# Recurrent mixer of a three-layer network: output products in runs, scores on 64 rows

## Chip, cores and metric

The kernel runs on one core of a Trainium2 chip. The metric is device time in microseconds: 3107.34 us, the median of 3 runs (3105.17 to 3111.62).

## What is computed

Input is a sequence of 512 tokens with 1024 features. A hybrid layer, an attention layer and a recurrent layer follow one another, each with an MLP. The change lies in the recurrent layer (RWKV-7), which runs over the tokens in both directions with 16 heads of 64 features each. Cut to its core:

```python
def rwkv7_scan(r, w, k, v, kk, a):
    def step(state, inp):
        r_t, w_t, k_t, v_t, kk_t, a_t = inp
        sa = jnp.einsum('bhvk,bhk->bhv', state, -kk_t)
        state = (state * w_t[:, :, None, :] + sa[..., None] * (kk_t * a_t)[:, :, None, :]
                 + v_t[..., None] * k_t[:, :, None, :])
        return state, jnp.einsum('bhvk,bhk->bhv', state, r_t)

for d in range(2):
    ...
    o = rwkv7_scan(*ins)
    ...
    dir_out.append((group_norm(o, gn_w, gn_b) + bonus.reshape(nB, S, D)) * g.astype(F32))
y = dir_out[0] + dir_out[1]
return y.astype(h.dtype) @ w_o
```

All of it is float32.

## The kernel before

The recurrent layer (`L3.rwkv`) takes the heads in pairs, so that one head lies on partitions 0 to 63 and the other on 64 to 127. A **unit** is one direction of one pair; there are 16, numbered 0 to 15 here. The 512 tokens of a unit are 8 chunks of 64. Three generators work on a unit:

- `prep` (L1265) makes the decays and the operands on DVE and ACT. Then come the **scores** (L1312): per head and chunk one product of `bk` (the chunk's b and k, 128 columns) with `ar`, masked by DVE (L1314) into `sc`. In `bk` the rows of the other head are zeros, so that each product has 128 rows. SP stores the diagonal blocks of the scores to DRAM (`lu`, L1321). PE also puts `bk` with tokens on the partitions (L1362, to `kb`).
- `invert` (L1367) reads `lu` back in another layout (`lt`, L1372, four DMAs) and inverts the triangular 32 x 32 blocks on POOL in 31 steps of two instructions (L1379, L1381). The result `x` goes out to DRAM (`xu`, L1388) and back into `X` (L1392), four DMAs each. `lt` and `x` have one buffer. PE finishes the 64 x 64 inverses (L1407, L1416).
- `scan` (L1423) builds the factors `m`, `n` (L1435 to L1457) and then runs the **chain** of states: per chunk one product a head (L1471) and one DVE instruction (L1472). Between the steps of the chain, `out` issues the **output** products of the chunk before into `po`: state products (L1465, 64 rows) and score-by-value products (L1467, 128 rows). The group norm (L1480 on), the gate and the sum follow. `lora2` (L1239) loads the gate's weight (128x128, one buffer) and splits it by ACT and DVE (L69, L70).

A loop over ticks advances every live generator by one step; a unit starts every 16 ticks, so that the scan of one unit, the inversion of the next and the preparation of the one after that run at the same time. Products of the values (L1207) and of the output weights (L1220) are mixed in. The emission order follows from the ticks, and a scheduling layer then places instructions on the queues; each engine and SP works through its own queue in order.

```python
for st, at in ((2, 36), (1, 9), (0, 0), (3, -4)):
    q, e = divmod(t - at, 16)
    if e == 0 and 0 <= q < NQ and not (st == 3 and q % 2):
        live.append((st, q, stages[st](q)))
```

Of the kernel before, what the change touches and what calls it, by code (L numbers as in the profile page):

```python
# [8 lines left out]
F32 = mybir.dt.float32  # L9
# [8 lines left out]
S = 512  # L18
# [6 lines left out]
class Core:  # L25
# [57 lines left out]
    def run(self, units, x, first=0, last=0, after=None, rate=1, segs=HALVES, before=None):  # L83
        """units: (weight AP [128, nk*128], consume(ps, s0, s1)); x[k] = (hi, lo) [128, S].
        The first and the last units run on half of the tokens at a time."""
# [22 lines left out]
    def final(self, units, x, put, g, then):  # L108
        """The last product of a block: put(m, a, ps) leaves tile m of its output in a; then
        h += norm(output) and the next norm start on one half of the tokens while the other half runs."""  # L110
# [26 lines left out]
    def ahead(self, gen, hp=HP):  # L137
        """The steps of gen, before what is already in the engines' queues."""
        if not hp:
            yield from gen  # L140
            return
        while True:
            with self.tc.high_priority(hp):
                try:
                    next(gen)
                except StopIteration:
                    return
            yield
# [15 lines left out]
    def prenorm(self, q, g, xn, s0, s1):  # L164
        """xn = h * rstd * g, split; q holds the squares of h."""
# [10 lines left out]
    def postnorm(self, y, q, g, s0, s1):  # L176
        """h += y * rstd * g; returns the squares of the new h."""
# [19 lines left out]
    def mlp(self, xn, g_post, w1, w2, ngrp, kind, then):  # L197
        """h += norm(act(xn @ w1) @ w2); w1(j) and w2(group, m) give packed weight APs."""
# [51 lines left out]
class SumSq:  # L250
    """Sum over the 1024 features (partitions of 8 tiles) of squares, spread over the partitions."""
# [59 lines left out]
class L1:  # L311
    """The hybrid mixer: sparse attention, spatial gating, RG-LRU, then the gated merge."""

    def l1_start(self, pool, xn, g):
        """Loads x and spawns the first norm; x is read again where it is added."""
# [65 lines left out]
    def branch(self, b, xn, x, merged, first=False):  # L381
        """merged += sigmoid(gate b) * (branch b @ its weights)."""
# [16 lines left out]
    # spatial gating  # L399

    def v_units(self, xn, v):
        """gelu(xn @ w_v) with the tokens on the partitions, 256 columns a step."""
# [61 lines left out]
    # RG-LRU  # L464
# [15 lines left out]
    def rglru(self, rg, xc):  # L480
        """Replaces each tile of xc by the recurrence's output."""
        nc, I = self.nc, self.I
        # rate = -8 softplus(-lam) = -8 (max(-lam, 0) + 2 atanh(e / (2 + e))), e = exp(-|lam|)
# [54 lines left out]
    # sparse attention: with 8 blocks and a window of the whole sequence, all three branches are causal  # L538

    def l1_attention(self, xn, g_pre, u, v):  # L540
        nc, tc, I = self.nc, self.tc, self.I
        yb = [self.accp.tile([128, S], F32, tag="acc", name="yb") for _ in range(NT)]
        with ExitStack() as cx:
# [27 lines left out]
            with tc.tile_pool(name="cm", bufs=1) as cm:  # L571
# [17 lines left out]
                def compress(which):  # L589
                    """The MLP over the blocks of 32 keys or values, 2 of a block's tokens at a time."""  # L590
# [89 lines left out]
            def compressed(hh, head, q, g, pct):  # L680
                """The branch over compressed blocks, for all of a head's queries."""
# [21 lines left out]
            def attend(pair, q, ks, vv, g):  # L703
                """A generator: the attention of a pair of heads of group g."""
# [104 lines left out]
class L2:  # L809
    """Dilated attention and windowed attention, then the output projection."""  # L810

    def bias_rows(self):
        """Bias of every distance and head, with the masks and the branches' multiplicities, in DRAM."""
# [16 lines left out]
    def q_split(self, ps, s0, s1, qst, scale, back=False):  # L830
        """Per head of a pair: its rows' high parts and, on the other 64 partitions, the low parts.
        With back the tokens run backwards."""
# [9 lines left out]
    def k_split(self, ps, s0, s1, krep):  # L842
        """Per head of a pair: high and low parts, each on both halves of the partitions."""
# [8 lines left out]
    def v_rows(self, vt, v):  # L852
        """v[:, b, :] = tokens of block b on the partitions."""
        nc = self.nc
        ps = self.pst.tile([128, 4, 128], F32, tag="tr", name="tr")
        for b in range(4):
            nc.tensor.transpose(ps[:, b, :], vt[:, b * 128:(b + 1) * 128], self.ident)
        nc.scalar.copy(v, ps)

    def l2_mixer(self, xn, g_post, then):  # L860
        nc, tc, I = self.nc, self.tc, self.I
        with ExitStack() as cx:
# [34 lines left out]
            def scores(pair, hh, qb, q, k, tb, win):  # L897
                """The weights of block qb of 128 queries of a head, which run backwards."""
# [29 lines left out]
            def attend(pair, q, ks, v, vc, win):  # L928
                """A generator: the attention of a pair of heads, in steps."""
# [80 lines left out]
class L3:  # L1010
    """The RWKV-7 mixer, in chunks of 64 tokens, both directions."""
# [19 lines left out]
    def l3_mixer(self, u, g_post, then):  # L1031
        nc, tc, I = self.nc, self.tc, self.I
        W = lambda n, i: I[n][i]
        with ExitStack() as lx:
# [3 lines left out]
            with tc.tile_pool(name="mx", bufs=8) as mx:  # L1038
# [5 lines left out]
                def blend(c, i, t, s0, s1):  # L1044
                    """A mix of the tokens before, at and after."""
# [82 lines left out]
    def rwkv(self, lp, rkd, vm, tw, ta, sg):  # L1128
        nc, tc, I = self.nc, self.tc, self.I
        with ExitStack() as cx:  # L1130
            pool = lambda n, b, **kw: cx.enter_context(tc.tile_pool(name=n, bufs=b, **kw))
            arp, vsp, bkp, unp, sp, wk = (pool(n, b) for n, b in (
                ("ar", 4), ("vs", 3), ("bk", 1), ("un", 1), ("s3", 2), ("wk", 2)))
# [24 lines left out]
            def head_scale(sq, fn):  # L1158
                """PSUM [128, S]: fn(sum over each head's 64 rows of sq), on all rows of the head."""
# [24 lines left out]
            def w4(i):  # L1184
                """A 4 KB tile out of the weights' slots."""
# [7 lines left out]
            # b and k, scaled by the inverse decays: (b, k) of the first head above zeros, (k, b) of the second below zeros  # L1193
            bk = bkp.tile([128, 2, 8, 2, 64], F32, tag="bk", name="bk")
            nc.gpsimd.memset(bk, 0.0)
# [3 lines left out]
            def values(p):  # L1199
                """The values of a pair of heads."""  # L1200
# [10 lines left out]
            def output(p):  # L1211
                """Adds a pair of heads' part of the output product."""
# [37 lines left out]
            def pair(p):  # L1250
                """What the two directions of a pair of heads share."""
# [16 lines left out]
            def prep(q, C):  # L1268
                """Decays, scores and the other operands of one direction of a pair of heads."""
# [24 lines left out]
                ar0, ar1 = ar[:, 0], ar[:, 1]  # L1294
                nc.vector.tensor_tensor(c8(ar0), c8(flip(kk, d)), dp[:, :, 0:64], op=ALU.mult)
                for h, rw, ow in H:
                    nc.vector.tensor_tensor(bk[rw, h, :, h, :], c8(al)[rw], c8(s)[rw], op=ALU.mult)
                yield
                nc.vector.tensor_tensor(kd, flip(k[p], d), kd, op=ALU.mult)
                for h, rw, ow in H:  # L1300
                    nc.vector.tensor_tensor(bk[rw, h, :, 1 - h, :], c8(kd)[rw], c8(s)[rw], op=ALU.mult)  # L1301
# [3 lines left out]
                sc = C["sc"] = []  # L1305
                for h, rw, ow in H:
                    sc.append(w4(h).rearrange("p (c t) -> p c t", c=8))
                    for g in range(2):
                        ps = self.psm.tile([128, 4, 2, 64], F32, tag="mm", name="mm")
                        for c in range(4):  # L1310
                            cc = 4 * g + c
                            nc.tensor.matmul(ps[:, c], bk[:, h, cc].rearrange("p a t -> p (a t)"),  # L1312
                                             ar[:, :, cc * 64:(cc + 1) * 64], start=True, stop=True)
                        nc.vector.tensor_tensor(sc[h][:, 4 * g:4 * g + 4, :], ps.rearrange("p c a t -> p c (a t)"),  # L1314
# [8 lines left out]
                # bonus, and the values centred over the head with the tokens on the partitions  # L1323
# [33 lines left out]
                # tokens on the partitions  # L1357
                kb = C["kb"] = w4(q % 2).rearrange("p (h c t) -> p h c t", h=2, c=8)
                for h, rw, ow in H:
                    ps = mm()  # L1360
                    for c in range(8):
                        nc.tensor.transpose(ps[:, c, :], bk[rw, h, c].rearrange("p a t -> p (a t)"),  # L1362
# [4 lines left out]
            def invert(q, C):  # L1367
                """Inverses of the 32 x 32 diagonal blocks: (quarter of the rows, unit) on the partitions;
                then the 64 x 64 ones."""
# [27 lines left out]
                # off-diagonal blocks: -X1 U12 X2  # L1397
# [25 lines left out]
            def scan(q, C):  # L1423
                """The recurrence of the states as S' = d (M S + n), one product a chunk, and the outputs
                S^T Q + [u0; v]^T scores; then the group norm and the gate."""
# [35 lines left out]
                def out(c):  # L1461
# [233 lines left out]
```

## Time and profile before

| | |
|---|---|
| median of 3 runs | 3107.34 us |
| profiled execution: span of its instructions | 3102.4 us |
| its own launch time | not listed by itself; the median is 4.9 us above the span |
| busy, share of the span | PE 95%, DVE 54%, ACT 43%, POOL 13% |
| recurrent stage | about 2031 to 2684 us |
| sum over 2028 to 2712 us | PE 611.3, DVE 369.8, ACT 273.1, POOL 360.8 us busy of 684 |

Busy shares are means over stages with different limits, so the stage is read by its own stretches, waits and timelines. In the rows below, x counts executed records; a float32 product of PE is two records. PEclk is the mean granted clock of TensorE as a share of 2.4 GHz. A row marked SPq is an issue of a DMA on SP's queue, PE a matmul. Times are from the span's start.

### The profile page before, as it was taken

What the parts mean: (1) busy time and instruction counts of PE and PEld (TensorE: products, weight loads), DVE (VectorE), ACT (ScalarE), POOL (GpSimd) and SP (SyncE); (2) the same over time, 40 slices, a digit from 0 to 9 for tenths busy, and PEclk for the clock granted to TensorE, in tenths of its full rate; (3) what the DMA queues carried; (4) which work ended last, traced back from release to release, by engine and by line L of the source; (5) the groups of instructions that cost most, each with busy time, mean ns of one, the idle gap of its engine ahead of it and who ended that gap; (6) DMA issues with size and microseconds to landing.
All of it is one profiled execution on the core that took longest, in us unless ns stands there. A gap on an engine that the chain in (4) does not pass through costs nothing.

```text
span 3102.4 us, 49534 instructions
## 1 busy us (share of the span) xinstructions
PE 2957.2 (95%) x19720; PEld 2382.2 (77%) x19720; DVE 1675.8 (54%) x3427; ACT 1344.1 (43%) x2450; POOL 397.6 (13%) x1117
## 2 busy tenths in 40 slices
PE   7999999999999999999999999979999999699998
PEld 7877778778888889777988897757666666488887
DVE  5566684553553335757733357855545555553345
ACT  5566652663443223555532235644444443243232
POOL 0000000000000000000000000045555555100000
PEclk9999999999999999999999999987889998899999
DMA  4301122223223223222222232311111111212231
GB/s 142 99 29 48 42 96 89 95 95 119 90 77 106 94 94 99 75 75 64 76 94 93 93 127 88 109 45 35 42 48 49 49 47 36 85 61 95 95 108 42
DMA packets 139415, 243.99 MB, mean 79 GB/s; under 512 B 62064, under 2 KB 82288, under 8 KB 139056
## 3 DMA queue, kind: packets, MB, share of 16 engines
q1 hardware_dynamic: 136864, 238.90, 24.5%
q8 instruction: 155, 2.54, 0.3%
q10 hardware_dynamic: 2320, 1.93, 0.2%
q14 instruction: 76, 0.62, 0.1%
HBM read 228.13 MB, written 12.65 MB: 78 GB/s over the span
## 4 chain that ended last, share of the span: by engine, by line
PE 80%; DVE 7%; POOL 4%; issue 3%; ACT 3%; DMA 2%; SPq 1%; POOLq 0%; ACTq 0%; DVEq 0%
PE mm L80 56%; PE fil L1207 2%; POOL x L1381 2%; POOL tmp L1379 2%; PE mm L1312 2%; PE fil L1220 2%; PE o L1467 2%; PE o L732 1%; PE mm L416 1%; PE o L1465 1%; PE mm L1090 1%; PE tr L722 1%; PE o L950 1%; PE mm L1248 1%; PE mm L761 1%
## 5 line engine op out<-in xcount | busy, mean ns | idle before, releaser
L80 PE MATMUL mm<-xh,wh 128*128 128x512 f32 (+1 forms) x2072 | 739.7, 358 | 10.7 <-ACT xh L69 6.6
L80 PE MATMUL mm<-xl,wh 128*128 128x512 f32 (+1 forms) x2072 | 736.5, 357 | 0.3 <-DVE xl L70 0.3
L80 PE MATMUL mm<-xh,wl 128*128 128x512 f32 (+1 forms) x2072 | 733.0, 355 | 2.1 <-DVE wl L65 2.1
L63 ACT CAST wh<-wr 128x1024 fp32r<-128x1024 f32 (+1 forms) x343 | 357.0, 1044 | 755.8 <-PE mm L80 612.1
L65 DVE TENSOR_TENSOR wl<-wr,wh 128x1024 fp32r<-128x1024 f32 (+1 forms) x343 | 416.6, 1216 | 458.8 <-ACT wh L63 448.9
L80 PEld LDWEIGHTS mm<-xh,wh 128*128 128x128 f32 x2072 | 392.7, 190 | 73.8 <-ACT xh L69 7.9
L80 PEld LDWEIGHTS mm<-xh,wl 128*128 128x128 f32 x2072 | 392.4, 190 | 60.8 <-issue 3.5
L80 PEld LDWEIGHTS mm<-xl,wh 128*128 128x128 f32 x2072 | 392.5, 190 | 56.6 <-issue 3.3
L80 PE MATMUL mm<-hl,wh 128*128 128x512 f32 (+1 forms) x880 | 304.9, 347 | 0.0
L80 PE MATMUL mm<-hh,wh 128*128 128x512 f32 (+1 forms) x880 | 303.6, 346 | 0.0
L80 PE MATMUL mm<-hh,wl 128*128 128x512 f32 (+1 forms) x880 | 303.5, 345 | 0.0
L1379 POOL TENSOR_TENSOR tmp<-x,lt 128x60 f32<-128x60 f32 (+24 forms) x496 | 170.6, 344 | 172.9 <-DMA lt<-lu 135.4
L275 POOL TENSOR_TENSOR r<-r,mhalf 128x2 f32<-128x2 f32 x24 | 24.1, 1003 | 1291.0 <-DVE r L274 1291.0
L80 PEld LDWEIGHTS mm<-hl,wh 128*128 128x128 f32 x880 | 166.4, 189 | 22.4 <-DVE hl L70 0.5
L80 PEld LDWEIGHTS mm<-hh,wl 128*128 128x128 f32 x880 | 166.2, 189 | 21.8
L80 PEld LDWEIGHTS mm<-hh,wh 128*128 128x128 f32 x880 | 166.1, 189 | 21.9
L1381 POOL TENSOR_TENSOR x<-x,tmp 128x60 f32<-128x60 f32 (+24 forms) x496 | 173.8, 350 | 38.9
L241 DVE TENSOR_TENSOR acc<-acc,mm 128x256 f32<-128x256 f32 (+1 forms) x88 | 47.4, 541 | 178.7 <-PE mm L80 178.7
L265 DVE TENSOR_TENSOR sqa<-sqa,sq 128x256 f32<-128x256 f32 x182 | 75.2, 421 | 56.1 <-ACT sq L264 52.2
L69 ACT CAST hh<-t 128x512 fp32r<-128x512 f32 (+1 forms) x106 | 57.0, 539 | 77.5 <-DVE t L212 68.4
L674 DVE CUSTOM_DVE_ANT_0 s<-mm,cmask 128x128 f32<-128x128 f32 (+3 forms) x128 | 59.9, 487 | 47.0 <-PE mm L756 23.1
L1312 PE MATMUL mm<-ar,bk 128*128 128x128 f32 x512 | 68.6, 291 | 15.1 <-DVE bk L1301 7.9
(399 smaller groups left out, 5010.1 us busy)
## 6 DMA issues: line engine op xcount, KB each, us to landing
wr<-in_mlp_w_dram SPq DMA_DIRECT2D x128, 512.0 KB, 3.5
wr<-in_w_ffn_in_dram SPq DMA_DIRECT2D x44, 512.0 KB, 3.5
wr<-in_w_mg_dram SPq DMA_DIRECT2D x24, 512.0 KB, 3.6
wr<-in_w_br_dram SPq DMA_DIRECT2D x24, 512.0 KB, 3.5
wr<-in_attn_w_in_dram SPq DMA_DIRECT2D x18, 512.0 KB, 3.6
wr<-in_w_ffn_out_dram SPq DMA_DIRECT2D x16, 512.0 KB, 3.5
lt<-lu SPq DMA_DIRECT2D x64, 128.0 KB, 2.6
wr<-in_w_kv_dram SPq DMA_DIRECT2D x12, 512.0 KB, 4.0
```

Of the source, the lines that this page charges most:

```text
L63: nc.scalar.copy(hi, raw)
L65: nc.vector.tensor_tensor(lo, raw, hi.bitcast(F32), op=ALU.subtract)
L69: self.nc.scalar.copy(hi, src)
L80: nc.tensor.matmul(ps, l, r[:, s0:s1], start=(n == 0), stop=(n == 3 * nk - 1))
L265: nc.vector.tensor_tensor(self.acc, self.acc, t, op=ALU.add)
L674: nc.vector.tensor_tensor_reduce(s, ps, mask, -1.0, 3e38, ADD, ALU.min, m)
L1207: nc.tensor.matmul(ps, w[:, i * 128:(i + 1) * 128], vm[i], start=(i == 0), stop=(i == NT - 1))
L1220: nc.tensor.matmul(ps, w[:, m], ys[p], start=True, stop=True)
L1312: nc.tensor.matmul(ps[:, c], bk[:, h, cc].rearrange("p a t -> p (a t)"), ar[:, :, cc * 64:(cc + 1) * 64], start=True, stop=True)
L1379: nc.gpsimd.tensor_tensor(t, x[:, :m, i:i + 1].to_broadcast([128, m, n]), lt[:, i:i + 1, i + 1:].to_broadcast([128, m, n]), op=ALU.mult)
L1381: nc.gpsimd.tensor_tensor(x[:, :m, i + 1:], x[:, :m, i + 1:], t, op=ALU.subtract)
L1467: nc.tensor.matmul(po[rw, c], sc[h][:, c, 64:128], vs[:, c, h, :], start=(c == 0), stop=True, skip_group_check=True)
```

## The change

Three edits. (1) `bk` holds both heads on their own 64 rows, (b, k) for the first and (k, b) for the second, without zeros; it is made anew per unit with two buffers, and the memset goes. A score product now reads 64 rows, and the products of the two heads follow each other chunk by chunk into two PSUM tiles. (2) All score-by-value products of a unit stand in one run ahead of the chain, with one more tick. (3) The state products follow the chain in the text. Elsewhere the diff takes out comments and docstrings only.

```diff
-                ("ar", 4), ("vs", 3), ("bk", 1), ("un", 1), ("s3", 2), ("wk", 2)))
+                ("ar", 4), ("vs", 3), ("bk", 2), ("un", 1), ("s3", 2), ("wk", 2)))
...
-            bk = bkp.tile([128, 2, 8, 2, 64], F32, tag="bk", name="bk")
-            nc.gpsimd.memset(bk, 0.0)
...
+                bk = bkp.tile([128, 8, 2, 64], F32, tag="bk", name="bk")
                 for h, rw, ow in H:
-                    nc.vector.tensor_tensor(bk[rw, h, :, h, :], c8(al)[rw], c8(s)[rw], op=ALU.mult)
+                    nc.vector.tensor_tensor(bk[rw, :, h, :], c8(al)[rw], c8(s)[rw], op=ALU.mult)
...
-                sc = C["sc"] = []
-                for h, rw, ow in H:
-                    sc.append(w4(h).rearrange("p (c t) -> p c t", c=8))
-                    for g in range(2):
-                        ps = self.psm.tile([128, 4, 2, 64], F32, tag="mm", name="mm")
-                        for c in range(4):
-                            cc = 4 * g + c
-                            nc.tensor.matmul(ps[:, c], bk[:, h, cc].rearrange("p a t -> p (a t)"),
-                                             ar[:, :, cc * 64:(cc + 1) * 64], start=True, stop=True)
-                        nc.vector.tensor_tensor(sc[h][:, 4 * g:4 * g + 4, :], ps.rearrange("p c a t -> p c (a t)"),
+                sc = C["sc"] = [w4(h).rearrange("p (c t) -> p c t", c=8) for h in range(2)]
+                for g in range(2):
+                    ps = [self.psm.tile([128, 4, 2, 64], F32, tag="mm", name="mm") for _ in range(2)]
+                    for c in range(4):
+                        cc = 4 * g + c
+                        for h, rw, ow in H:
+                            nc.tensor.matmul(ps[h][:, c], bk[rw, cc].rearrange("p a t -> p (a t)"),
+                                             ar[rw, :, cc * 64:(cc + 1) * 64], start=True, stop=True)
+                    for h in range(2):
+                        nc.vector.tensor_tensor(sc[h][:, 4 * g:4 * g + 4, :], ps[h].rearrange("p c a t -> p c (a t)"),
                                                 mask.unsqueeze(1).to_broadcast([128, 4, 128]), op=ALU.mult)
...
-                def out(c):
-                    cs = slice(c * 64, (c + 1) * 64)
+                for c in range(8):
                     for h, rw, ow in H:
-                        if c:
-                            nc.tensor.matmul(po[rw, c], ar1[rw, cs], n[rw, c - 1, :], start=True, stop=False,
-                                             skip_group_check=True)
-                        nc.tensor.matmul(po[rw, c], sc[h][:, c, 64:128], vs[:, c, h, :], start=(c == 0), stop=True,
+                        nc.tensor.matmul(po[rw, c], sc[h][:, c, 64:128], vs[:, c, h, :], start=(c == 0), stop=False,
                                          skip_group_check=True)
+                yield
                 for c in range(1, 7):
...
-                    out(c - 1)
                     yield
-                out(6)
-                out(7)
+                for c in range(1, 8):
+                    for h, rw, ow in H:
+                        nc.tensor.matmul(po[rw, c], ar1[rw, c * 64:(c + 1) * 64], n[rw, c - 1, :], start=False, stop=True,
+                                         skip_group_check=True)
```

The queues move at two places that the prediction speaks of. The first is SP's queue around the gap after unit 8 (lines in the changed program stand 1 to 3 lower; `lora_dram 128x128` is the gate's weight). Before:

```order
L1214 DMA wr<-in_rk_w_o_dram 128x8x128
L1254 DMA k<-rkd 128x512
L1255 DMA r<-rkd 128x512
L1388 DMA xu<-x 256x1x32 x2
L1321 DMA lu<-wh 32x8x32 x2
L1388 DMA xu<-x 256x1x32 x2
L1241 DMA w_22618<-in_rk_lora_dram 128x128
L1321 DMA lu<-wl 32x8x32 x2
L1241 DMA w_23078<-in_rk_lora_dram 128x256
L1392 DMA X<-xu 32x8x32 x4
L1372 DMA lt<-lu 32x1024 x4
```

And in the changed program:

```order
L1238 DMA w_23079<-in_rk_lora_dram 128x256
L1251 DMA k<-rkd 128x512
L1252 DMA r<-rkd 128x512
L1238 DMA w_22633<-in_rk_lora_dram 128x128
L1387 DMA xu<-x 256x1x32 x4
L1320 DMA lu<-wh 32x8x32 x2
L1320 DMA lu<-wl 32x8x32 x2
L1391 DMA X<-xu 32x8x32 x4
L1371 DMA lt<-lu 32x1024 x4
```

The four xu now stand together, the lu behind them, and both weights have moved ahead of xu.

The second is PE's queue at the start of the last unit's chain (sc is the chain's PSUM tile, o the outputs'). Before:

```order
L1471 MATMUL sc_25482<-n,m 64x64 x2
L1467 MATMUL o_25481<-vs,wh 64x64
L1467 MATMUL o_25481<-vs,wl 64x64
L1465 MATMUL o_25481<-n,ar 64x64
L1467 MATMUL o_25481<-vs,wh 64x64
L1465 MATMUL o_25481<-n,ar 64x64
L1471 MATMUL sc_25482<-n,m 64x64 x2
L1467 MATMUL o_25481<-vs,wl 64x64
L1465 MATMUL o_25481<-n,ar 64x64
L1467 MATMUL o_25481<-vs,wh 64x64
L1465 MATMUL o_25481<-n,ar 64x64
L1467 MATMUL o_25481<-vs,wl 64x64
```

And in the changed program, from the end of the run of 16 score-by-value products:

```order
L1463 MATMUL o_25495<-vs,wh 64x64
L1463 MATMUL o_25495<-vs,wl 64x64
L1468 MATMUL sc_25496<-n,m 64x64 x2
L1473 MATMUL o_25495<-n,ar 64x64 x2
L1468 MATMUL sc_25496<-n,m 64x64 x2
L1473 MATMUL o_25495<-n,ar 64x64 x2
L1468 MATMUL sc_25496<-n,m 64x64 x2
L1473 MATMUL o_25495<-n,ar 64x64 x2
```

The score-by-value products (L1463) have left the chain; the state products (L1473) stand between its steps in pairs, and four come behind the last step.

## Rows read from the trace of the kernel before

**Rows 1.** Busy time by stretch: engine busy us (x instructions), PEclk, DMA share, GB/s.

```profile
2180.00:2218.00 38.00, 31.81 (x415) 24.68 (x414) 19.35 (x37) 20.48 (x35) 21.87 (x64) 0.77 0.16 40
2370.00:2408.00 38.00, 37.98 (x485) 27.36 (x485) 23.99 (x49) 14.35 (x27) 21.43 (x59) 1.00 0.19 46
```

**Rows 2.** Waits from 2020 to 2720 us: engine, line, releaser; us, times, longest.

```profile
POOL tmp L1379 <- DMA lt<-lu: 135.4, 16, 36.5
POOL x L1374 <- DMA xu<-x: 70.9, 15, 5.4
```

**Rows 3.** Waits of SP's own queue from 2100 to 2600 us, same columns.

```profile
SPq L1388 <- POOL x L1381: 186.9, 12, 27.3
SPq L1321 <- DVE n L1472: 2.0, 4, 1.3
```

**Rows 4.** Timeline of POOL, units 8, 9, 15: start us, us, engine, line, op, tiles.

```profile
2345.55 0.24 POOL L1379 TENSOR_TENSOR tmp<-x,lt 128x31 f32<-128x31 f32 x1 [6.90 <-DMA lt<-lu]
...
2377.74 0.40 POOL L1374 COPY x<-xeye 128x256 f32<-128x256 f32 x1 [5.36 <-DMA xu<-x]
...
2385.50 0.24 POOL L1379 TENSOR_TENSOR tmp<-x,lt 128x31 f32<-128x31 f32 x1 [6.90 <-DMA lt<-lu]
...
2393.28 0.29 POOL L1379 TENSOR_TENSOR tmp<-x,lt 128x60 f32<-128x60 f32 x1
...
2401.64 0.62 POOL L1379 TENSOR_TENSOR tmp<-x,lt 128x60 f32<-128x60 f32 x1
...
2622.27 0.24 POOL L1379 TENSOR_TENSOR tmp<-x,lt 128x31 f32<-128x31 f32 x1 [7.94 <-DMA lt<-lu]
...
2645.97 0.21 POOL L1381 TENSOR_TENSOR x<-x,tmp 128x8 f32<-128x8 f32 x1
```

**Rows 5.** Timeline of SP's issues in the gaps after units 5 and 8.

```profile
2255.39 2.90 SPq L1388 DMA_DIRECT2D xu<-x  x4
...
2262.64 1.73 SPq L1372 DMA_DIRECT2D lt<-lu  x4
...
2372.40 1.22 SPq L1388 DMA_DIRECT2D xu<-x  x2
...
2376.36 0.53 SPq L1241 DMA_DIRECT2D w<-in_rk_lora_dram  x1
...
2381.34 1.78 SPq L1372 DMA_DIRECT2D lt<-lu  x4
```

**Rows 6.** Timeline of PE in the stage: scores, a run of products, alternating products.

```profile
2327.98 1.95 PE L1312 MATMUL mm<-ar,bk 128*128 128x128 f32 x16
2329.86 1.03 PE L1445 MATMUL mm<-vs,wh 128*64 128x64 f32 x28
...
2336.18 0.33 PE L1467 MATMUL o<-vs,wh 128*64 128x64 f32 x2
2336.44 0.32 PE L1465 MATMUL o<-n,ar 64*64 64x64 f32 x2
```

**Rows 7.** Timeline of DVE near the end of unit 8's inversion.

```profile
2370.09 0.68 DVE L1314 TENSOR_TENSOR wh<-mm,const 128x512 f32<-128x512 f32 x1
2370.69 0.34 DVE L70 TENSOR_TENSOR w<-w,w 128x128 fp32r<-128x128 f32 x1
```

**Rows 8.** Timeline of the last unit's chain of states, PE, DVE and ACT.

```profile
2665.93 0.33 PE L1471 MATMUL sc<-n,m 64*64 64x64 f32 x4
...
2668.97 0.33 PE L1471 MATMUL sc<-n,m 64*64 64x64 f32 x4
...
2669.36 0.28 DVE L1472 SCALAR_TENSOR_TENSOR n<-sc,dl,n 128x64 f32<-128x64 f32 x1 [1.27 <-PE sc L1471]
...
2671.93 0.48 PE L1471 MATMUL sc<-n,m 64*64 64x64 f32 x4
...
2672.46 0.28 DVE L1472 SCALAR_TENSOR_TENSOR n<-sc,dl,n 128x64 f32<-128x64 f32 x1 [1.54 <-PE sc L1471]
...
2677.30 0.60 ACT L1480 ACTIVATE t<-o 128x512 f32<-128x512 f32 x1 [13.67 <-PE o L1467]
```

More of the change, by code (lines that the diff above doesn't have):

```diff
@@ L1300, in prep @@
                 for h, rw, ow in H:
-                    nc.vector.tensor_tensor(bk[rw, h, :, 1 - h, :], c8(kd)[rw], c8(s)[rw], op=ALU.mult)
+                    nc.vector.tensor_tensor(bk[rw, :, 1 - h, :], c8(kd)[rw], c8(s)[rw], op=ALU.mult)
                 nc.vector.tensor_tensor(c8(ar1), c8(flip(r[p], d)), dp[:, :, 1:65], op=ALU.mult)
@@ L1361, in prep @@
                     for c in range(8):
-                        nc.tensor.transpose(ps[:, c, :], bk[rw, h, c].rearrange("p a t -> p (a t)"),
+                        nc.tensor.transpose(ps[:, c, :], bk[rw, c].rearrange("p a t -> p (a t)"),
                                             self.ident[rw, rw])
```

## Prediction

> **What bounds the kernel now.** I read three views in this order: the busy time by stretch, who waits for whom, and the timelines of POOL and SP. All of the change lies in the recurrent mixer, where PE seems to be the limit: from 2370 to 2408 us it is busy 37.98 of 38 us [rows 1]. The waits say otherwise. There are 16 units (a direction of a pair of heads, 0 to 15). Per unit POOL inverts triangular blocks in 62 instructions, and between two inversions it waits first for the store of its result (xu), then for the next unit's input (lt) [rows 2]. SP, which issues both, waited in its queue almost only for POOL's result; for scores (lu) it waited 2.0 us behind the costliest entry [rows 3]. So a ring closes without PE: POOL inverts, SP issues xu, X and lt in turn, POOL starts again. For unit 8 the inversion runs from 2345.55 until xu is issued at 2372.40 (26.8 us), and the next starts at 2385.50: a gap of 13.1 us, 12.3 of them waits and the rest POOL's own work [rows 4, 5]. Over the 15 gaps: (135.4 - 36.5 for the first unit + 70.9) / 15 + 0.9 = 12.2 us [rows 2]. A period is thus about 39 us, with no instruction of PE in it.
>
> The test is a stretch in which PE has less to do. From 2180 to 2218 it is busy only 31.8 of 38 us, at a mean granted clock of 0.77 [rows 1], and POOL is as busy (21.9 against 21.4 us). PE idling or not, the ring turns alike. What PE saves inside the ring is therefore covered by the inversion. Three places remain: the start, SP's part of the ring, and the tail after the last inversion.
>
> **PE's saving, and what it is worth inside.** *Scores.* 32 records of 128 columns (two records per product) take 2 x 1.95 us a unit [rows 6]. On 64 rows, with the heads taken alternately, I expect two products side by side: 1.95 us saved, or 0 if they run one after another. *Scan.* 30 output products a unit change the array's shape from one to the next, one every 0.26 us (2336.18 to 2336.44): 30 x 0.26 = 7.8 us. In one run the same kind costs 1.03 / 28 = 0.037 us a record, so 60 records are 2.2 us; with about eight changes of shape left at 0.26 - 0.07 = 0.19 it is 3.7 us. Saved: 4.1 us. Together 6 us a unit, 97 us over 16 units. All of it is hidden in the ring; if that cover were gone it would show in full (first rival).
>
> **The start.** Unit 0's scores stand ahead of the ring. PE finishes up to 1.95 us sooner, but DVE must still mask four tiles, now two at a time. Bounds 0 and 1.95 us. A mask takes 0.68 us [rows 7]: two finished tiles after 0.97 us and four masks give 3.7 us, where four tiles at 0.97 us and the last mask give 4.6. I take 0.9.
>
> **SP's part of the ring.** The change moves more than it says. In the gap after unit 8, SP issues two xu, two lu, two xu, a small weight, two lu, another weight, then X and lt. In the changed order four xu stand first, and both weights have moved ahead of them, under the inversion. What this is worth is read from unit 5, which has the good order already: from xu to lt 2262.64 - 2255.39 = 7.25 us, against 2381.34 - 2372.40 = 8.94 [rows 5]. A clean gap is then 13.1 - 1.7 = 11.4 us, 0.8 under the mean. In the changed program ten of the 15 gaps have xu first (after units 4 to 9 and 11 to 14), though three of these keep a weight inside (0.53 us of issue); after units 2, 3 and 10 the xu are still split, and after unit 1 the lu move ahead of the ring. I take ten times 0.7, 7 us. Bounds: 0, if the stretching of single issues takes it back, and 13, if every one of the ten has been at 12.7.
>
> Moved past on SP are also the loads of k, r and the output weights, now ahead of xu in several units. They wait for slots that PE, ACT or DVE free, and behind them waits the ring; see the third rival.
>
> **The tail.** Behind the last inversion nothing hides PE. The last unit's chain takes from 2665.93 to 2677.30, 11.4 us [rows 8], with outputs between its six steps. After: a run of 32 score records, 32 x 0.037 = 1.2 us. Then six steps, each from PE's start to DVE's start 0.39, DVE 0.28, and back to PE at least 0 and at most the same 0.39, of which I take 0.1: 0.77, so 4.6 us, with the state products inside them; the last four products 0.3. That is 6.1 us, 5.3 less. At the lower clock a step is 0.53 + 0.28 + 0.1 = 0.9 us, and with the products doubled I get 8.4 us, 3.0 less. The same four records grow from 0.33 to 0.48 us between 2669 and 2672, and with less work before them they may stand at the lower clock from the first step. I take 4.3 between. The Trainium skill ("TensorE: Matmul & The Clock Gate", section "HAM oscillation — how this bites in real kernels") warns of just this: pauses of TensorE bring its clock down, so saved work can be paid back in rate. By it the sum would take the 3.0; [rows 1] agree with it: 0.77 where PE idles, 1.00 where it does not.
>
> **Sum.** 0.9 + 7 + 4.3 = 12.2 us. The profiled span is 3102.4 us, 4.9 under the median of 3107.3; so 3090.2 in the profile and **3095.1 us** as median. From the bounds: 0 + 0 + 3 = 3 us to 2 + 13 + 5.3 = 20 us saved, 3087 to 3104. A measurement of this kernel tells 0.2% (6.2 us) from no change.
>
> **Rivals.** *First, PE is the bound after all.* For: the full stretch of [rows 1]. Against: the ring of [rows 2, 3], in which PE has no part. Time: 97 + 4 us less, 3006. Chance 0.05.
>
> *Second, POOL gives it back.* The inversion is not of one length: 26.8 us for unit 8, 23.9 for unit 15, behind which no preparation runs [rows 4]. One form of POOL's takes 0.29 us at 2393 and 0.62 at 2401, while DVE prepares a unit. If PE is ready sooner, DVE's work gathers right behind X, inside the inversion, and its own waiting moves into the gap. The dearest case is that all of DVE's work falls inside: 2.9 us go with what now overlaps, some 27/39 of it, so at most 2.9 x 12/27 = 1.3 us a unit, 19 us. A typical half, 10 us, leaves 12.2 - 10 = 2 us: 3105, no change. The Trainium skill ("SBUF — State Buffer", section "Who interferes with whom") gives the rule: a VectorE instruction with two SBUF inputs holds up a GpSimd instruction that reads SBUF. [...] Chance 0.18.
>
> *Third, slower: a load holds up SP.* In the gaps after units 4, 6, 8, 12 and 14 a small weight (128x128) now stands directly ahead of xu, and it waits until DVE has split the weight before it. In unit 8 that split ends at 2371.03 [rows 7], 1.4 us before xu at 2372.40. The point that decides is the inversion's end: each us by which the split comes later lengthens the ring by one. If in these five units it came 6 us behind the inversion, 30 us are added, and 3107.3 + 30 - 12 = 3125. Against it: what leads to the split is PE work of the unit before, which gets shorter by up to 6 us. Chance 0.05.
>
> *That the change doesn't do what it says*, the 64-row products not running side by side, alters only the start and stays inside the forecast.
>
> **Numbers.** The forecast has 0.72, the rivals 0.05, 0.18 and 0.05. The range 3085 to 3106 holds the forecast with both its bounds and most of the second rival; outside lie the first, the third and the worst of the second. Faster by over 0.2% (below 3101.1): nine tenths of the forecast, the first rival, and a sixth of the second: 0.65 + 0.05 + 0.03 = 0.73. Slower: the third, and a little of the second: 0.06. Between: 0.21.
>
> **What would show it.** Right: PE's busy time in the stage falls by 60 us or more while POOL's inversions keep their 26 to 27 us and 62 instructions; xu to lt takes 7.3 to 8 us; the last chain ends within 9 us; the output products lie in runs at under 0.05 us a record. Score records start at half the spacing where heads alternate; equal spacing would show that step wrong. Wrong altogether would be a period far below 36 us (PE or DVE had set it), or SP waiting at the small weight with xu's data ready.

## Result and the profile after

| | before | after |
|---|---|---|
| median, runs taken side by side | 3106.26 us (4 runs, 3104.9 to 3111.62) | 3078.55 us (4 runs, 3076.38 to 3079.8) |
| span of the profiled execution | 3102.4 us | 3074.6 us |

The ratio is 0.991, interval 0.989 to 0.993: 27.7 us less, where the prediction had 12.2. The direction was right; the time lies 6 us below the low end of the range.

The busy time by stretch, in the changed kernel (columns as in [rows 1]); the last row is the stretch of the table of before, 611.3 us of PE there:

```profile
2180.00:2218.00 38.00, 25.60 (x431) 20.05 (x431) 17.50 (x36) 18.27 (x33) 20.58 (x64) 0.81 0.20 49
2360.00:2398.00 38.00, 27.76 (x293) 17.16 (x293) 18.05 (x35) 13.97 (x23) 22.91 (x66) 0.78 0.16 39
2028.00:2712.00 684.00, 538.83 (x7260) 390.04 (x7259) 386.91 (x774) 296.38 (x538) 352.31 (x1026) 0.84 0.20 51
```

PE lost 72.5 us of busy time in the stage, and in 17 stretches of 38 us from 2040 us on it is busy for 36.1 us at most (37.98 before); POOL is about as busy as before (352.3 us, before 360.8). The waits of POOL from 2020 to 2720 us and of SP from 2100 to 2600 us, against [rows 2, 3]:

```profile
POOL tmp L1378 <- DMA lt<-lu: 120.1, 14, 39.0
POOL x L1373 <- DMA xu<-x: 67.9, 15, 6.0
...
SPq L1387 <- POOL x L1380: 169.1, 10, 23.6
SPq L1387 <- POOL X L1384: 88.3, 4, 29.4
SPq L1320 <- DVE n L1469: 0.7, 2, 0.4
```

They read as before: POOL waits for xu, then lt, SP for POOL. One inversion and the gap behind it (POOL, then SP, then the masks of the next unit on DVE), unit 8 as in [rows 4, 5]:

```profile
2339.82 1.35 POOL L1378 TENSOR_TENSOR tmp<-x,lt 128x31 f32<-128x31 f32 x1 [7.14 <-DMA lt<-lu]
...
2364.75 0.21 POOL L1380 TENSOR_TENSOR x<-x,tmp 128x8 f32<-128x8 f32 x1
2369.01 0.40 POOL L1373 COPY x<-xeye 128x256 f32<-128x256 f32 x1 [4.05 <-DMA xu<-x]
...
2376.05 0.24 POOL L1378 TENSOR_TENSOR tmp<-x,lt 128x31 f32<-128x31 f32 x1 [6.18 <-DMA lt<-lu]
```
```profile
2364.99 2.52 SPq L1387 DMA_DIRECT2D xu<-x  x4
2367.62 1.03 SPq L1320 DMA_DIRECT2D lu<-wh  x2
2368.74 0.89 SPq L1320 DMA_DIRECT2D lu<-wl  x2
2369.90 1.78 SPq L1391 DMA_DIRECT2D X<-xu  x4
2371.84 1.72 SPq L1371 DMA_DIRECT2D lt<-lu  x4
```
```profile
2352.24 0.69 DVE L1313 TENSOR_TENSOR wh<-mm,const 128x512 f32<-128x512 f32 x1 [0.52 <-PE mm L1310]
2352.85 0.68 DVE L1313 TENSOR_TENSOR wl<-mm,const 128x512 f32<-128x512 f32 x1
```

The inversion takes 25.1 us, the gap 11.1 (26.8 and 13.1 before); xu to lt is 6.9 us. The last mask is done at 2353.5, 11.4 us ahead of the inversion's end. Now the same masks in the kernel before, where this inversion ended at 2372.4 [rows 5]:

```profile
2372.92 0.69 DVE L1314 TENSOR_TENSOR wl<-mm,const 128x512 f32<-128x512 f32 x1
2373.81 0.69 DVE L1314 TENSOR_TENSOR wl<-mm,const 128x512 f32<-128x512 f32 x1 [0.20 <-PE mm L1312]
```

They came 2.1 us **after** the end, and waited for PE's scores. The prediction never compared these two times.

Worked out from the timelines of POOL, DVE and ACT, over the whole stage:

| us | before | after | change |
|---|---|---|---|
| stage's first norm (kk) to the first inversion | 21.5 | 22.2 | +0.6 |
| 16 inversions | 421.2 | 410.7 | -10.5 |
| 15 gaps | 182.6 | 171.2 | -11.5 |
| last inversion's end to the square of the outputs (ACT) | 31.1 | 25.7 | -5.4 |
| median end of the last mask against the inversion's end, units 7 to 14 | 0.0 | -9.9 | |

These parts are 26.8 of the spans' 27.8 us. The rest lies ahead of kk (+1.0) and behind the tail (-2.0), in code that is the same; over all profiles of this study kk begins between 2019.4 and 2024.7 us, and what follows the tail takes 422.7 to 425.1, so nothing is read into it.

The tail, PE, DVE and ACT in the last unit's chain ([rows 8] before):

```profile
2645.55 0.27 PE L1463 MATMUL o<-vs,wh 128*64 128x64 f32 x1
...
2646.64 0.33 PE L1468 MATMUL sc<-n,m 64*64 64x64 f32 x4
2647.02 0.28 DVE L1469 SCALAR_TENSOR_TENSOR n<-sc,dl,n 128x64 f32<-128x64 f32 x1 [0.73 <-PE sc L1468]
2647.36 0.33 PE L1468 MATMUL sc<-n,m 64*64 64x64 f32 x4 [0.27 <-DVE n L1469]
...
2650.95 0.48 PE L1473 MATMUL o<-n,ar 64*64 64x64 f32 x4 [0.27 <-DVE n L1469]
2651.48 0.60 ACT L1478 ACTIVATE t<-o 128x512 f32<-128x512 f32 x1 [8.32 <-PE o L1473]
```

From the run of outputs to ACT 5.9 us, a step 0.72 us.

### The profile page after: what moved, and what is told of

The parts are those of the page before. It is cut to its first block, busy times and chain, and to the rows that moved or that the text cites. A ratio compares the mean times of both kernels' runs of the same rounds, so it can differ in the third digit from the quotient of the medians.

```text
span 3074.6 us, 49553 instructions
## 1 busy us (share of the span) xinstructions
PE 2859.1 (93%) x19720; PEld 2302.1 (75%) x19720; DVE 1671.7 (54%) x3427; ACT 1356.4 (44%) x2460; POOL 386.7 (13%) x1116
## 4 chain that ended last, share of the span: by engine, by line
PE 74%; POOL 9%; DVE 6%; issue 4%; DMA 3%; ACT 2%; SPq 2%; POOLq 0%; ACTq 0%; DVEq 0%
PE mm L80 57%; POOL x L1380 4%; POOL tmp L1378 4%; PE o L732 1%; PE mm L416 1%; PE mm L1090 1%; PE tr L722 1%; PE o L950 1%; PE fil L1204 1%; DMA lt<-lu 1%; PE mm L761 1%; PE tr L924 1%; DVE sqa L265 1%; PE mm L903 1%; SPq L1391 1%
## 5 line engine op out<-in xcount | busy, mean ns | idle before, releaser
L80 PEld LDWEIGHTS mm<-hh,wh 128*128 128x128 f32 x880 | 166.2, 189 | 21.8
L241 DVE TENSOR_TENSOR acc<-acc,mm 128x256 f32<-128x256 f32 (+1 forms) x88 | 47.4, 541 | 178.3 <-PE mm L80 178.3
L70 DVE TENSOR_TENSOR hl<-t,hh 128x512 fp32r<-128x512 f32 (+1 forms) x106 | 62.2, 589 | 35.3 <-ACT hh L69 34.6
```

Source lines behind the costliest of these rows:

```text
L70: self.nc.vector.tensor_tensor(lo, src, hi.bitcast(F32), op=ALU.subtract)
L80: nc.tensor.matmul(ps, l, r[:, s0:s1], start=(n == 0), stop=(n == 3 * nk - 1))
L241: nc.vector.tensor_tensor(a, a, ps, op=ALU.add)
```

## Experiments

Eleven kernels ran, each beside the kernel before on one chip. In e1 to e4 the prediction's **ring** stood against **PE** (the gain is a share of what PE saved). Their results led to a third theory, **two limits**: before the change PE's work and the ring of POOL and SP were of equal length from unit 7 on, so each took back what the other was given; the change freed PE, and the ring alone remained.

| run | median us | ratio to before, interval | inversions / gaps, us | last mask, units 7 to 14 |
|---|---|---|---|---|
| e1 scores edit alone | 3109.87 | 0.9998, 0.9986 to 1.001 | 412.0 / 200.6 | +4.0 |
| e2 scan edit alone | 3083.74 | 0.9909, 0.9895 to 0.9923 | 415.6 / 173.9 | -8.2 |
| e3 before, half of POOL's steps | 3079.06 | 0.9899, 0.988 to 0.9918 | | |
| e4 after, half of POOL's steps | 2971.60 | 0.9549, 0.9536 to 0.9562 | | |
| e5 before, lu on ACT's queue | 3110.80 | 1.0013, 0.9999 to 1.0026 | 420.7 / 183.6 | +3.1 |
| e6 after, lu on ACT's queue | 3092.81 | 0.9958, 0.9945 to 0.997 | 418.5 / 178.3 | -4.7 |
| e7 after, two buffers, lu and lt on ACT | 3125.03 | 1.0065, 1.0051 to 1.0078 | 422.3 / 208.0 | -0.6 |
| e8 after, one-input products | 3043.33 | 0.9797, 0.9782 to 0.9812 | 383.4 / 170.5 | -8.9 |
| e9 after, lu first | 3033.68 | 0.9754, 0.9733 to 0.9776 | 412.5 / 125.0 | -2.5 |
| e10 after, ring open | 3078.41 | 0.9894, 0.9874 to 0.9914 | 421.4 / 162.2 | +3.1 |
| e11 before, lu first | 3124.40 | 1.0047, 1.003 to 1.0065 | 415.7 / 204.9 | +5.8 |

(Last column: median end of a unit's last mask against the end of the running inversion; plus is late.)

### Which edit: e1 and e2

e1 is the changed kernel with the scan's old text, e2 the kernel before with the new scan and the old scores.

> The scores edit alone: the scan keeps its old text, outputs between the steps of the chain. SP's queue has the four xu together in 13 of 15 gaps, as in the full change. Theory 'ring' (POOL's inversion and SP's issues set the period, the tail is separate): the gaps shrink by 7 to 12 us, the inversions by some us, the last chain stays at 11.4 us; 10 to 17 us less than before, 3089 to 3096. Rival 'PE' (PE's readiness sets the period, and the gain is a share of PE's saved time): the scores give about a quarter of the 72 us that PE saved, so a quarter of the 28 us: 7 us less, 3099, whatever SP's order is.

> The scan edit alone: outputs in one run and behind the chain, scores as before on 128 rows with zeros. xu stays split by lu in 8 of the gaps. Theory 'ring': the tail gives 5.4 us, the gaps 0 to 4 us and the inversions 0 to 5 us: 6 to 12 us less, 3094 to 3100. Rival 'PE': three quarters of the saved PE time lie here, so three quarters of the 28 us, about 21 us less, 3085.

The scan edit alone gives the whole gain, some 28 us, where PE's share had three quarters of it; the scores edit gives none, which neither theory had. In e1 the scores took PE 45.0 us in the stage (2028 to 2712 us) instead of 68.6, but PE's busy time there stayed the same, 610.9 us (611.3 before), at a lower granted clock, 0.82 instead of 0.85. From 2300 to 2500 us PE was full at 0.81 (0.91 before, first of the four rows of the next section):

```profile
2300.00:2500.00 200.00, 196.45 (x2107) 132.91 (x2106) 106.75 (x210) 77.23 (x140) 107.34 (x318) 0.81 0.17 44
```

So PE gained nothing from the smaller scores there; why the clock was lower is not shown. e1 has the four xu together, and its inversions are as short as in the changed kernel, but its gaps add up to 200.6 us. From unit 7 on the masks are late. The worst gap, behind unit 7's inversion, on POOL, SP and DVE:

```profile
2326.52 0.21 POOL L1380 TENSOR_TENSOR x<-x,tmp 128x8 f32<-128x8 f32 x1
2338.32 0.40 POOL L1373 COPY x<-xeye 128x256 f32<-128x256 f32 x1 [11.59 <-DMA xu<-x]
2348.88 0.24 POOL L1378 TENSOR_TENSOR tmp<-x,lt 128x31 f32<-128x31 f32 x1 [9.69 <-DMA lt<-lu]
```
```profile
2333.80 0.33 SPq L1238 DMA_DIRECT2D w<-in_rk_lora_dram  x1
2334.22 2.52 SPq L1387 DMA_DIRECT2D xu<-x  x4
2339.07 1.63 SPq L1320 DMA_DIRECT2D lu<-wh  x2
```
```profile
2338.95 0.68 DVE L1313 TENSOR_TENSOR wl<-mm,const 128x512 f32<-128x512 f32 x1
```

SP stands at the gate's weight until 2333.8, and xu comes 7.5 us late: the third rival, here and, by 2.1 us, behind unit 9. Then lu waits for a mask that ends at 2339.6, 12.9 us behind the inversion. This gap is 22.2 us. With the masks late, the better order on SP bought nothing.

### Which limit: e3 and e4

```diff
                 for i in range(31):
+                    if i % 2 == 0:
+                        continue
                     m, n = i // 4 + 1, 31 - i
```

> The kernel before with every second step of POOL's inversion left out (15 of 31 steps remain, so the states are computed from a wrong inverse). Each inversion becomes some 13 us shorter. Theory 'ring': the period falls from 39.2 us until PE is full; PE's busy time is 554 of the ring's 604 us, at a mean clock of 0.85, so 45 to 90 us less, 3015 to 3060. Rival 'PE' (PE paced the stage before): under 15 us less, above 3090.

> The changed kernel with the same steps left out. Theory 'ring': the period falls until PE is full, and PE's busy time is 470 of 582 us: 100 to 150 us less than the changed kernel, 2930 to 2980, so the change is worth 70 to 95 us once POOL is out of the way. Rival 'PE': the change already got what PE had to give; the two kernels with half of the steps stand 28 us apart as the full ones do.

Half of the steps are some 16 x 13 = 208 us of POOL. Before the change this brought 32 us, between the two expectations; after it 107 us, as the ring had it, and the two stand 107.5 us apart instead of 28. PE from 2300 to 2500 us says why. In the fence: before, changed kernel, e3, e4.

```profile
2300.00:2500.00 200.00, 193.62 (x2246) 137.28 (x2246) 113.84 (x220) 82.44 (x151) 114.40 (x320) 0.91 0.19 49
```
```profile
2300.00:2500.00 200.00, 174.46 (x2382) 117.82 (x2381) 122.82 (x238) 93.72 (x167) 119.39 (x341) 0.90 0.20 51
```
```profile
2300.00:2500.00 200.00, 196.10 (x2298) 137.53 (x2298) 113.10 (x222) 82.18 (x149) 48.74 (x160) 0.91 0.19 48
```
```profile
2300.00:2500.00 200.00, 194.49 (x2915) 136.74 (x2909) 139.23 (x274) 105.65 (x188) 74.91 (x194) 0.98 0.25 61
```

Before, PE was full already (193.6 of 200) and stayed so in e3. After, it has 25 us of 200 free, and e4 fills them. So halving POOL's work alone gave 32 us, and freeing PE alone 28. Where e3's 32 us lie, the first DVE instruction of the chain tells, in units 7 and 13, before and in e3:

```profile
2375.32 0.28 DVE L1472 SCALAR_TENSOR_TENSOR n<-sc,dl,n 128x64 f32<-128x64 f32 x1
...
2609.79 0.28 DVE L1472 SCALAR_TENSOR_TENSOR n<-sc,dl,n 128x64 f32<-128x64 f32 x1
```
```profile
2355.82 0.28 DVE L1474 SCALAR_TENSOR_TENSOR n<-sc,dl,n 128x64 f32<-128x64 f32 x1
...
2589.95 0.28 DVE L1474 SCALAR_TENSOR_TENSOR n<-sc,dl,n 128x64 f32<-128x64 f32 x1
```

From one to the other a unit takes 39.1 us before and 39.0 in e3: from unit 7 to 13 PE set the pace, and half of POOL's work made no difference. The gain lies elsewhere: of 28 us, counted from kk in the two profiles, 10 are there by the chain of unit 0, 21 by that of unit 7, 22 by that of unit 13, and the rest comes behind it. In the changed kernel a unit takes 37.8 us between the same two places, and 31.6 in e4, so there the ring is the limit. From unit 7 on the two limits were thus not equal, but close: PE's was the longer, by some 1.3 us a unit. What PE's saving is worth without POOL in the way is 107 us; the prediction's first rival had 97 + 4.

### The order on SP: e5, e6 and e7

```diff
-                        nc.sync.dma_start(lu[u0:u0 + 8].rearrange("c s t -> s c t"),
+                        nc.scalar.dma_start(lu[u0:u0 + 8].rearrange("c s t -> s c t"),
```

> The kernel before with the store of the scores (lu, four DMAs a unit) issued from ACT's queue instead of SP's: between two inversions SP issues xu, X and lt alone, and the four xu stand together. This is the SP term of the prediction by itself. Theory 'SP order' (the prediction's): the 15 gaps shrink by 7 to 13 us in all, 3095 to 3100. Theory 'two limits' (before the change PE's work was as long as the ring from unit 7 on, so that the masks came at the end of the inversion): what the gaps lose is given back as lateness of the masks, and the time stays within 5 us of before.

> The same edit in the changed kernel, where the masks are 2 to 16 us ahead of the inversion's end. Theory 'two limits' (after the change the ring alone is the limit): SP's gap shortens in full. X can be issued 4.0 us after the first xu (as it was behind the last inversion, where no lu stands between), against 4.7 now in a clean gap and 6.2 to 6.7 in four: 0.7 us in some ten gaps and 2 us in four, 10 to 15 us less than the changed kernel, 3063 to 3069. Rival (PE is the limit in the changed kernel as well): within 5 us of it.

e7 does the same with lt, and gives lt and x two buffers and bk one.

> The changed kernel with the ring opened: lt and x get two buffers each (bk one, for the room), and lu and lt are issued from ACT's queue, so that POOL finds the next unit's input waiting and needs no xu before it starts. The gap should fall from 11.4 us to about 1 us. Theory 'two limits': POOL would need 27 us a unit, so PE becomes the limit at the time that the run with half of POOL's steps showed, 2971.6 us; 2965 to 3000. Rival: ACT, which then waits for the landing of lu in its own queue, delays the preparation, 3010 to 3060.

e5 agrees with two limits: with only xu, X and lt left on SP, the 15 gaps stay at 183.6 us, and the time within 0.3%. It does not show the prediction's SP term by itself, though, for the move has a price of its own: ACT's copy of the values waits up to 14.9 us for xu (25.7 us in 3) and 62.3 us in 7 for lu, and PE waits 9.2 us for the copy, which it did not do before. e6 came 24 us above its range and e7 65 us above even the rival's, for the reason that e7's rival named, only dearer: the move holds up ACT. The waits from 2020 to 2720 us, e6 first, then e7:

```profile
ACT vs L1337 <- DMA xu<-x: 57.5, 4, 19.3
ACT vs L1337 <- DMA lu<-wh: 46.3, 7, 10.4
...
PE mm L1352 <- ACT vs L1337: 40.6, 11, 9.2
```
```profile
ACT vs L1337 <- DMA xu<-x: 46.8, 3, 24.1
ACT vs L1337 <- DMA lu<-wh: 31.8, 9, 10.4
...
PE mm L1352 <- ACT vs L1337: 69.0, 15, 14.8
```

ACT's copy of the values (L1337) stands behind the new DMA issues; these wait for landings, xu's among them, up to 19 and 24 us, and PE waits for the copy, as it does not in the changed kernel. So e7 says nothing on what an open ring is worth, and e6 nothing on SP's 0.7 us; both show what a waiting DMA issue costs on an engine that computes.

### Why the inversions got shorter: e8

In `prep`, the products with two SBUF inputs on six lines (eight instructions a unit, not seven as the expectation counts) became scalings with one, for example:

```diff
-                    nc.vector.tensor_tensor(bk[rw, :, h, :], c8(al)[rw], c8(s)[rw], op=ALU.mult)
+                    nc.vector.tensor_scalar_mul(bk[rw, :, h, :], c8(al)[rw], 1e-3)
```

> The changed kernel with the seven products of a unit's preparation that read two SBUF operands on DVE (al, kd, ar twice, bk four times) replaced by one-input scalings of the same shape; the factors that they multiply in are left out, so the decays no longer enter. Theory 'DVE against POOL' (DVE's two-input operations hold up POOL; that is why the inversions were shorter where this work fell into the gap): all inversions fall to 24 us, as the last one has, 411 to 385 us in all, and the time by 18 to 27 us, 3051 to 3061. Rival (the inversions' length comes from elsewhere): sum of the inversions 405 to 415 us, time within 5 us of the changed kernel.

The inversions came to 383.4 us (385 expected), 27.3 less; the gaps stayed within 0.7 us of the changed kernel's. The time fell by 35 us, more than the 18 to 27: the shorter preparation also brought the first inversion 4.5 us closer to kk. One form of POOL's instructions by shape (x, mean ns) from 2100 to 2600 us, before, after, e8:

```profile
L1379 POOL TENSOR_TENSOR tmp<-x,lt 128x60 f32<-128x60 f32 x38 | 16.0, 422 | 3.0
```
```profile
L1378 POOL TENSOR_TENSOR tmp<-x,lt 128x60 f32<-128x60 f32 x39 | 13.4, 344 | 3.1
```
```profile
L1378 POOL TENSOR_TENSOR tmp<-x,lt 128x60 f32<-128x60 f32 x42 | 12.9, 306 | 3.3
```

So DVE's preparation holds up POOL. Where it lies, the timelines tell: of these six lines and the next product (L1323 after the change), 96.5 of 98.1 us lay inside inversions before and 84.5 of 96.3 after. PE is done sooner, so the preparation of every second unit begins in the gap; the inversions of units 2, 4, ... 14 take 25.0 us, those of 3, 5, ... 13 as before 26.6. The Trainium skill ("SBUF — State Buffer", section "Who interferes with whom") states that a VectorE instruction with two SBUF inputs holds up a GpSimd instruction that reads SBUF; e8 agrees, 27.3 us in 16 inversions. The scalings are also shorter, 0.44 us against 0.70, so e8 bounds the effect of the second input from above; it does not isolate it. The timelines tell more: beside these two-input products alone, an instruction of POOL's inversion takes on average 0.35 us longer than the shortest of its shape (74 records of the changed kernel), beside the scalings alone 0.10 us (57 records of e8), and with DVE idle less than 0.01. So the scalings hold up POOL too, but less.

### A better order: e9, e10 and e11

e9 puts lu ahead of xu and lt behind it by a dependence: two tiny POOL instructions at an inversion's end add a zero made from the next unit's last masked tile; X is issued a tick later; the gate's weight gets two buffers.

```diff
+                if q + 1 < NQ:
+                    z = unp.tile([128, 1], F32, tag="z", name="z")
+                    nc.gpsimd.tensor_scalar(z, Cs[q + 1]["sc"][1][:, 7, 0:1], 0.0, None, ALU.mult)
+                    nc.gpsimd.tensor_tensor(x[:, 0, 0:1], x[:, 0, 0:1], z, op=ALU.add)
                 X = C["x"] = self.hp.tile([128, 8, 64], F32, tag="h", name="X")
...
                     nc.sync.dma_start(xu[:, :, f, :], x[32 * f:32 * f + 32])
+                yield
```

> The changed kernel with another order on SP and nothing on ACT: two small POOL instructions at the end of an inversion make xu wait for the next unit's masks, so that lu stands ahead of xu in every gap; X is issued a tick later, so that lt stands directly behind xu; the gate's weight gets two buffers. Between xu and lt remain the 2.6 us of issuing xu, against 6.9 in a clean gap now, and POOL starts 4.2 us after lt: a gap of 6.9 us instead of 11.4. Theory 'two limits' (the ring alone binds in the changed kernel): 15 x 4.5 us less, about 3010, or up to 3030 where odd units' masks (2 to 6 us ahead of the end) come late. Rival (PE or the landing of DMAs takes it back): 3065 to 3080.

> The same, and lt loaded in the preparation into one of two buffers, ahead of xu on SP, with two buffers of x (bk has one): at an inversion's end POOL finds its next input in place. The gap falls to some 2 us, a period could be 28 us, and PE becomes the limit. Theory 'two limits': the time of the run with half of POOL's steps, 2971.6 us, within 15 us. Rival: with xu held until the next lt has landed, X and the scan come later, and PE waits there: 3000 to 3050.

> The kernel before with the edits of e9. The gap could fall as much, but theory 'two limits' says that PE, full from unit 7 on, stops it where the run with half of POOL's steps did, at 3079.1 us or above, since xu now waits for masks that come late: 3079 to 3106. Then the change is worth 60 us or more under this order, twice what it is under the old one. Rival (the ring alone set the time before): 3107 - 67 = 3040.

e9 beats both kernels: some 45 us below the changed one, 2.5% below the kernel before, and 4 us above its range. The gaps fell from 171 to 125 us, the best to 7.3. SP around unit 5's inversion, which ends at 2239.3:

```profile
2234.25 1.03 SPq L1320 DMA_DIRECT2D lu<-wh  x2
2235.37 0.89 SPq L1320 DMA_DIRECT2D lu<-wl  x2
2239.79 2.56 SPq L1391 DMA_DIRECT2D xu<-x  x4
2242.51 1.88 SPq L1371 DMA_DIRECT2D lt<-lu  x4
```

lu is out before the inversion ends, and lt 2.7 us behind xu. e9 stops short of 3010, in part because the tiny instructions put 0.5 us into almost every gap, and because xu comes 1.9, 4.1 and 2.5 us behind the end of the inversion in units 8, 10 and 12: the masks, now 2.5 us ahead, are late again by 0.6 and 1.5 us in units 8 and 10.

The same edits on the kernel before make it slower, by 0.5%. POOL shows it directly, since its tiny instruction waits for the masks (e11, one of them, then the sum from 2020 to 2720 us):

```profile
2254.93 0.22 POOL L1386 TENSOR_SCALAR z<-wl 128x1 f32<-128x1 f32 x1 [10.97 <-DVE wl L1314]
...
POOL z L1386 <- DVE wl L1314: 74.9, 11, 12.3
```

Its time is 18 us above the expected range. That holding xu for the masks delays X, and with it the scan and PE, is a reading and not tested; the granted clock of the stage was lower as well, 0.82 against 0.85. e10 went the rival's way and 28 us beyond it: with xu held until the next lt has landed (POOL's tiny instruction waits 138.6 us for that, in 14 gaps), the masks come up to 13 us late, and nothing is gained over the changed kernel. e10 also leaves bk one buffer, and no run parts the two. An open ring without such a hold was tried in e7 alone, where ACT was held up.

## Why the prediction was half right

**The ring.** Right for the changed kernel: POOL's waits read as forecast, e2 and the changed kernel have the same ratio to before (0.991), although the scores cost PE 17 us more in e2, and e9 gains where SP's order improves. Wrong for the kernel before, and this is the step that failed: "so a ring closes without PE", and "all of it is hidden in the ring". It was tested on one early stretch (2180 to 2218 us), where the masks were some 11 us ahead. From unit 7 on they came at or behind the inversion's end, PE was full, and a period (inversion and gap) took 39.5 us instead of 37.6 in units 0 to 6. SP's 2.0 us of waiting for lu [rows 3] hid this: lu stood behind xu in the queue, and by the time its turn came the late mask had mostly arrived. e3 shows that PE set the pace there (39.1 us a unit in the chain, 39.0 with half of POOL's steps), so its saving showed until the ring, at 37.8, became the limit; only the rest was hidden.

**PE's saving.** Forecast 6 us a unit. Busy time inside the ring: scores 64.9 to 48.0 us, 1.1 us a unit instead of 1.95; outputs 127.7 to 51.5 us, 5.1 instead of 4.1. Together 6.2. Sixteen score records fell from 1.95 to 1.16 us, so two products do run side by side; the run of 32 output records took 1.09 us, 0.034 each.

**The start.** Forecast 0.9 less, measured 0.6 more. The last lu was issued 0.4 us sooner counted from kk, but lt waited 2.7 us behind it instead of 1.3. e1 with the new scores took 22.3 us from kk, e2 with the old ones 21.8: no gain here.

**SP's part.** Forecast 7, measured 11.5 in the gaps, inside its bounds. That the size is near is luck, for the order was not the main reason: in e2, where lu still stands between the xu in eight gaps, the gaps add up to 173.9 us, 8.7 less than before, and in e1, where the four xu stand together in every gap, to 200.6. The gaps got shorter mainly with the scan edit, which brought the masks early. xu to lt took 6.9 us in the clean gaps, below the 7.3 to 8 given.

**The inversions.** No term; measured -10.5 us. The second rival had the mechanism and the wrong sign: it took DVE's products as spread over the period (27/39 inside), when 96.5 of 98.1 us lay inside inversions already. Nothing could gather there; it could only leave.

**The tail.** The working gave 6.1 us, the chain took 5.9; then 4.3 was taken instead of 5.3, since the chain might start at the lower clock, and 5.4 came. It started at the full clock, which fell only at the end (the chain in the changed kernel):

```profile
2646.00:2650.00 4.00, 2.88 (x66) 2.12 (x60) 1.52 (x6) 0.00 (x0) 0.00 (x0) 1.00 0.63 218
2650.00:2651.50 1.50, 0.93 (x12) 0.60 (x12) 0.46 (x2) 0.02 (x1) 0.00 (x0) 0.74 0.00 0
```

Over the whole chain the mean was 0.92 (2646.6 to 2651.5 us), against 0.68 before (2666.0 to 2677.3), although PE now pauses 0.27 us in each step and was busy for 10.98 of 11.3 us before. The Trainium skill ("TensorE: Matmul & The Clock Gate", section "HAM oscillation — how this bites in real kernels") tells of TensorE waiting for data and starting the next work at the lower clock; this stretch does not show it, as the chain started at 1.00.

**The first and the third rival.** PE was the bound, but not alone, so 97 us became 28; e3 and e4 give back the 107. The small weight did not hold up xu in the changed kernel, where the first xu is issued 0.03 us after every inversion, and did in e1.

## What to carry to other kernels

Before calling one loop the bound, compare, late in the stage and not only early, when each side's product is ready with when the other side takes it; a producer that finishes just as it is asked for shows almost no wait. Where two loops are of nearly one length, an edit to the longer is worth only the distance to the other, and the next edit has to go to the other side: the same reordering of SP gave 45 us with PE freed and cost 15 us without. A store that is ready early should stand ahead of the one that waits, on a queue that computes nothing.

## What the runs showed that was not expected

PE's clock fell in both forms of the last chain, some 4 us behind its first step. Before, PE was busy for all 7.00 us from 2670 to 2677 us at a mean granted clock of 0.51, about the lower of its two levels (1.2 GHz), after 3 us at 1.00 (2666 to 2669 us, busy for 2.72), and four chain records took 0.48 us instead of 0.33. After, the clock stood at 1.00 until 2650 us, and when it fell, the shorter chain was all but over. In e1 a lower clock went with a saving on PE that did not show in its busy time. Scalings with one input, at 0.44 us, still held up POOL, by less than a third of what the two-input products did (0.10 us against 0.35 for an instruction beside them). And moving four small DMAs a unit to ACT's queue cost up to 19 us in one wait (24 with four more).
